# Splitting two late stores into halves in a channel shuffle kernel bound by its DMA engines

## The chip, the cores and the metric

The kernel runs on one core of a Trainium2 chip. The metric is the device time of one execution in microseconds (us), as a median of several runs. A ratio of two kernels is the mean time of one kernel's fast runs over that of the other's of the same rounds, with a 95% interval; it is not quite the ratio of the medians that are quoted. Executions over 1.5% slower than the fastest of the same kernel are left out of the means. A gain or loss counts as such from 2% on. Single times of a trace are given to 0.01 us, some of them cut and not rounded.

## The reference, cut to what matters

```python
batch, h, w, c = 16, 64, 64, 256
groups = 8
x = x.reshape(batch, h, w, groups, c // groups)
x = x.transpose(0, 1, 2, 4, 3)          # (group, channel) -> (channel, group)
return x.reshape(batch, h, w, c)        # float32
```

The input has 67.11 MB and the output as many. Each pixel's 256 channels are permuted; nothing is added or multiplied.

## The kernel before

```python
_SIZES = [4, 8, 16] + [32] * 15 + [4]     # pixels of each of 128 partitions in a tile
_IN_BUFS = 3
_OUT_BUFS = 3
...
    first = 0
    for q in _SIZES:
        in_tile = in_pool.tile([P, biggest * c], F32, name="in_tile")
        nc.sync.dma_start(out=in_tile[:, : q * c], in_=rows(x_flat, first, q))
        out_tile = out_pool.tile([P, biggest * c], F32, name="out_tile")
        nc.vector.tensor_copy(
            out=out_tile[:, : q * c].rearrange("p (i j g) -> p i j g", j=CPG, g=G),
            in_=in_tile[:, : q * c].rearrange("p (i g j) -> p i j g", g=G, j=CPG),
        )
        nc.scalar.dma_start(out=rows(out_flat, first, q), in_=out_tile[:, : q * c])
        first += P * q
```

There are 19 tiles, numbered from 0. SyncE issues a load for each, VectorE copies it with the permutation, and ScalarE issues its store. A partition of a full tile (q = 32) is one row of 32 KB that is contiguous in memory; a tile with q = 4 has rows of 4 KB. Below, L18 and S18 are the load and the store of tile 18.

Of the kernel before, what the change touches and what calls it, by code (L numbers as in the profile page):

```python
# [1 line left out]

# [4 lines left out]


F32 = mybir.dt.float32
P = 128  # L10

_SIZES = [4, 8, 16] + [32] * 15 + [4]
_IN_BUFS = 3
_OUT_BUFS = 3


@with_exitstack
def kernel(  # L18
    ctx: ExitStack,
    tc: tile.TileContext,  # L20
    x: bass.AP,
    groups: bass.AP,
    out: bass.AP,
):
    nc = tc.nc
    b, h, w, c = x.shape
    G = int(groups)
    CPG = c // G
    assert G * CPG == c
    assert sum(_SIZES) * P == b * h * w  # L30
    biggest = max(_SIZES)

    x_flat = x.rearrange("b h w c -> (b h w c)")
    out_flat = out.rearrange("b h w c -> (b h w c)")

    in_pool = ctx.enter_context(tc.tile_pool(name="in_pool", bufs=_IN_BUFS))
    out_pool = ctx.enter_context(tc.tile_pool(name="out_pool", bufs=_OUT_BUFS))

    def rows(flat, first, q):

        return flat[first * c : (first + P * q) * c].rearrange("(p f) -> p f", p=P)

    ctx.enter_context(tc.manual_schedule(engines=None))
    first = 0
    for q in _SIZES:
        in_tile = in_pool.tile([P, biggest * c], F32, name="in_tile")
        nc.sync.dma_start(out=in_tile[:, : q * c], in_=rows(x_flat, first, q))  # L47
        out_tile = out_pool.tile([P, biggest * c], F32, name="out_tile")
        nc.vector.tensor_copy(  # L49
            out=out_tile[:, : q * c].rearrange("p (i j g) -> p i j g", j=CPG, g=G),  # L50
            in_=in_tile[:, : q * c].rearrange("p (i g j) -> p i j g", g=G, j=CPG),
        )
        nc.scalar.dma_start(out=rows(out_flat, first, q), in_=out_tile[:, : q * c])
        first += P * q


# [1 line left out]
_INS = ['x', 'groups']  # L58
_OUTS = [((16, 64, 64, 256), 'float32')]

_NUMBERS = {'groups': 8}


# [26 lines left out]
```

## Time and profile before

| What | Value | Where it is read |
|---|---|---|
| time | 316.96 us (316.69 to 317.02, 3 runs) | runs |
| span of the profiled run | 315.2 us | page, headline |
| two DMA queues | 49.8% + 49.4% of 16 engines | page, DMA queues |
| VectorE | 38% busy | page, busy shares |
| L18, issue to landing | 42.1 us | chain of waits |
| S18, issue to landing | 14.9 us | DMA issues from 299.2 us on |

The page's part on DMA issues gives, for each kind of DMA, the queue, the count, the size and the median time from issue to landing:

```profile
in_tile<-in_x_dram SPq DMA_DIRECT2D x15, 4096.0 KB, 50.5
out_dram<-out_tile ACTq DMA_DIRECT2D x15, 4096.0 KB, 42.4
```

A full tile is 4096 KB and would take 4.19 MB / 432 GB/s = 9.7 us alone. That it takes 42 to 50 us says that several stand in line on each queue.

### The profile page before, as it was taken

The numbers are of one execution on the slowest core, as the hardware profiler recorded it, in microseconds if no ns is written. First come the engines' busy times: TensorE is split into PE (matmuls) and PEld (weight loads), VectorE is DVE, ScalarE is ACT, GpSimd is POOL, SyncE is SP. The second block draws the span as 40 slices with busy tenths as digits, with TensorE's granted clock in tenths as the row PEclk, the third lists the DMA queues.
The fourth block names the chain that finished last, engine by engine and source line by source line (L and its number), as shares of the span: only waits on it lengthen the run. The fifth ranks groups of instructions, "written<-read, shape, count | busy, mean of one in ns | idle before, by whom it ended". The sixth has DMA issues, their size and how long they took to land.

```text
span 315.2 us, 150 instructions
## 1 busy us (share of the span) xinstructions
DVE 119.9 (38%) x19; POOL 0.2 (0%) x4
## 2 busy tenths in 40 slices
DVE  2419270905318062270722608135090440905500
POOL 0000000000000000000000000000000000000000
DMA  8999999999999999999999999999999999999996
GB/s 314 408 422 458 403 449 408 457 408 453 412 453 412 458 412 453 420 445 428 437 428 437 437 428 437 428 437 433 437 433 437 428 441 424 445 420 426 439 441 291
DMA packets 5472, 134.22 MB, mean 426 GB/s; under 512 B 608, under 2 KB 608, under 8 KB 1120
## 3 DMA queue, kind: packets, MB, share of 16 engines
q1 hardware_dynamic: 2736, 67.11, 49.8%
q10 hardware_dynamic: 2736, 67.11, 49.4%
HBM read 67.11 MB, written 67.11 MB: 426 GB/s over the span
## 4 chain that ended last, share of the span: by engine, by line
DMA 40%; another core or an unknown queue 30%; DVE 25%; issue 0%; DVEq 0%; SPq 0%
DMA in_tile<-in_x_dram 40%; DVE out_tile L49 25%; DVEq L49 0%; SPq L47 0%
## 5 line engine op out<-in xcount | busy, mean ns | idle before, releaser
L49 DVE COPY out_tile<-in_tile 128x8192 f32<-128x8192 f32 (+3 forms) x19 | 119.9, 6313 | 179.3 <-DMA in_tile<-in_x_dram 179.3
L71 POOL MEMSET const-uint8-127<- 128x1 uint8 x1 | 0.1, 103 | 0.0
L71 POOL MEMSET const-bfloat16-1.0<- 128x1 bf16 x1 | 0.1, 102 | 0.0
L71 POOL MEMSET const-float32-0.0<- 128x1 f32 x1 | 0.1, 99 | 0.2 <-issue 0.2
L71 POOL MEMSET const-float32-1.0<- 128x1 f32 x1 | 0.1, 99 | 0.0
## 6 DMA issues: line engine op xcount, KB each, us to landing
in_tile<-in_x_dram SPq DMA_DIRECT2D x15, 4096.0 KB, 50.5
out_dram<-out_tile ACTq DMA_DIRECT2D x15, 4096.0 KB, 42.4
in_tile<-in_x_dram SPq DMA_DIRECT2D x1, 2048.0 KB, 11.1
out_dram<-out_tile ACTq DMA_DIRECT2D x1, 2048.0 KB, 30.1
in_tile<-in_x_dram SPq DMA_DIRECT2D x2, 512.0 KB, 22.7
in_tile<-in_x_dram SPq DMA_DIRECT2D x1, 1024.0 KB, 5.5
out_dram<-out_tile ACTq DMA_DIRECT2D x2, 512.0 KB, 14.4
out_dram<-out_tile ACTq DMA_DIRECT2D x1, 1024.0 KB, 22.9
```

The costliest lines, as they stand in the source:

```text
L49: nc.vector.tensor_copy(out=out_tile[:, : q * c].rearrange("p (i j g) -> p i j g", j=CPG, g=G), in_=in_tile[:, : q * c].rearrange("p (i g ...
L71: nc = _bacc.Bacc("TRN2", target_bir_lowering=False, num_devices=1)
```

## The change

Its intent is that the last large stores leave in smaller pieces, so that the small load and store behind them get through earlier.

```diff
+_HALVED = (16, 17)
...
-    for q in _SIZES:
+    for t, q in enumerate(_SIZES):
...
-        nc.scalar.dma_start(out=rows(out_flat, first, q), in_=out_tile[:, : q * c])
+        n = 2 if t in _HALVED else 1
+        for k in range(n):
+            cols = slice(k * q // n * c, (k + 1) * q // n * c)
+            nc.scalar.dma_start(
+                out=rows(out_flat, first, q)[:, cols], in_=out_tile[:, cols]
+            )
```

## The prediction

> **What bounds the kernel now.** I read the page's headline and busy shares first, then the forty slices, the table of DMA queues, the groups by shape, the DMA issues, and at the end the chain of waits.
>
> ```profile
> span 315.2 us, 150 instructions
> DVE 119.9 (38%) x19; POOL 0.2 (0%) x4
> DMA  8999999999999999999999999999999999999996
> q1 hardware_dynamic: 2736, 67.11, 49.8%
> q10 hardware_dynamic: 2736, 67.11, 49.4%
> ```
>
> VectorE, the only engine that computes, is busy for 38% of the span. The DMA engines are at 9 tenths or more in every slice but the first and the last, and the two queues (q1 carries the loads, q10 the stores) together fill 49.8 + 49.4 = 99.2% of sixteen engines' time. So the kernel is bound by its DMA engines: 134.22 MB go through them and nothing else counts unless it leaves them without work.
>
> The stretches at the end, cut at the times that matter below (columns: stretch, its length, busy DVE, busy POOL, clock, DMA share, GB/s), say that this holds until the last two microseconds:
>
> ```profile
> 280.00:287.00 7.00, 0.00 (x0) 0.00 (x0) 1.00 1.00 432
> 287.00:292.40 5.40, 5.17 (x1) 0.00 (x0) 1.00 1.04 445
> 292.40:298.00 5.60, 2.30 (x1) 0.00 (x0) 1.00 0.99 424
> 298.00:303.00 5.00, 1.09 (x1) 0.00 (x0) 1.00 1.00 433
> 303.00:312.40 9.40, 0.00 (x0) 0.00 (x0) 1.00 0.94 407
> 312.40:315.20 2.80, 0.00 (x0) 0.00 (x0) 1.00 0.32 132
> ```
>
> The share stays at 0.94 to 1.04 up to 312.4 us; there is no gap that an earlier store could fill. The last stretch holds the small last store, its landing and the closing barrier.
>
> The chain of waits ends with a piece that looks like a target for this change:
>
> ```profile
> 255.96 42.12 DMA in_tile<-in_x_dram
> 298.08 0.03 issue
> 298.11 0.05 DVEq L49
> 298.15 0.04 issue
> 298.20 1.09 DVE out_tile L49
> ```
>
> The load of the last, small tile (512 KB) is issued at 255.96 and lands only at 298.08. I number tiles from 0, as the code does: tile 18 is this one, tiles 16 and 17 are the ones whose stores are halved, L and S are loads and stores. The landing records of the trace (sixteen semaphore steps for each DMA; I quote the ninth as the middle and the sixteenth as the last) give L17 at 287.15 last, so 10.9 us pass between two landings for 512 KB. The DMA records explain it: one record of a 32 KB row takes 1213 ns on its engine, one of 4 KB 159 ns, and each engine takes one row of the load queue and one of the store queue in turn. L18 has 8 rows of 4 KB on each engine: 8 x (0.159 + 1.213) = 10.98 us. But while it waits its turn the engines move store rows, so this wait costs the bound nothing.
>
> **What the Trainium skill says.** "DMA: Bandwidth & Descriptors", section "Queues, rings and completion order", has each DMA engine go round-robin between the queue rows at the granularity of packets, of several descriptors. The trace agrees on the taking of turns and shows turns of a single row: besides the 10.9 us above, S1 (8 KB rows) and S2 (16 KB rows) landed beside loads of 32 KB rows 14.82 us apart in the middle, and 8 x (0.611 + 1.213) = 14.59. The same page, "Where 436 GB/s comes from", puts the ceiling at 435 GB/s; here a 32 KB row in 1213 ns is 27.0 GB/s for an engine, 432 for sixteen, which is the 432 of the stretch above. Its section "Why small descriptors are slow" tells of a fixed cost for each packet: the trace has medians of 159, 309, 611 and 1213 ns for 4, 8, 16 and 32 KB, so a row cut in two costs 2 x 611 - 1213 = 9 ns more. "Trainium Kernel Development and Optimization", "Key Constraints", says that DMAs from all issuing engines share the same 16 DMA engines; the shares of q1 and q10 add up to 99.2% here, which agrees.
>
> **The change part by part.** Removed: two stores of 4096 KB with rows of 32 KB. Added: four of 2048 KB with rows of 16 KB. No byte, VectorE instruction or load is added.
>
> Part 1, **time on the DMA engines**. On each engine 16 rows of 1213 ns (two stores, 8 rows each) become 32 rows of 611 ns: 16 x 9 = 144 ns more. Two more DMAs mean two more semaphore writes on each engine, 9 ns each by the records: 18 ns. Sum: +0.16 us, all of it on the bound, as the engines have no gap.
>
> Part 2, **the issues**. Two more store issues on ScalarE's queue, each of 338 to 380 ns. S16 is issued at 275.3, and its rows start after S15's middle landing at 292.40; S17 is issued at 294.73, and its rows start after S16's middle landing at 302.76. So the second halves are in the queue some 7 to 16 us before their turn. Cost: 0.
>
> Part 3, **new waits**. The built program uses eight DMA semaphores in turn, and two DMAs more shift those after them. By the order of instructions with their waits, the halves wait for old loads and for S12 and S14, the last of which landed at 279.03: done before the issues that name them. One is real: L18 now also waits for S13, which landed at 259.63, where it was issued at 255.96. It goes out 3.7 us later. Its rows can move only after L17's, whose middle landing is 286.83: 27 us of slack. Cost: 0.
>
> Part 4, **the taking of turns**. This is the visible gain. Up to S15's end at 292.40 L18 makes (292.40 - 286.83) / 1.372 = 4 of its 8 turns against 32 KB rows, as before. The other 4 are now beside 16 KB rows: 4 x (0.159 + 0.611) = 3.08 us in place of 4 x 1.372 = 5.49. L18 should land 2.4 us earlier, near 295.7, VectorE should then copy tile 18 from about 295.8 to 296.9 (it ends tile 17 at 294.7, so it is free), and S18 should be issued at about 296.9 and not at 299.31. But S18 stands behind S17 in the same queue, and S17's rows run until 312.44. What is gained is more waiting in the queue. Gain at the end: 0.
>
> Part 5, **the closing waits**. SyncE waits at the end for the eight semaphores in four pairs. Before, S18's was in the second pair, so two pairs were still to be passed after its landing at 314.21, about 62 ns each by the trace. In the changed program it is in the last pair: -0.12 us.
>
> Sum: +0.16 + 0 + 0 + 0 - 0.12 = +0.04 us. 316.96 + 0.04 = **317.0 us**.
>
> **The rivals.**
> - *The earlier last store shortens the end.* It would be 2.4 us if S18's issue at 299.31 set the end: 314.6 us, 0.8% faster, and still within 2%. For it speaks the chain of waits, which ends at tile 18's copy. Against it speaks that S18's issue takes 14.9 us to land, for 512 KB which need 8 x 0.159 = 1.27 us on an engine, and that the share stays near 1 from 298 to 312.4. I give it 4%.
> - *Shorter rows lose bandwidth.* A row's record is measured at 611 ns only for S2, beside loads. If 16 KB pieces with a pitch of 32 KB wrote 10% slower to HBM, 8.4 MB at 432 GB/s are 19.4 us, so +1.9 us: 318.9 us. For it: the pieces of a half aren't contiguous, as S2's rows are. Against: a row is still 16 KB long, and 8 KB rows reach 309 ns, 98% of the rate of a long row. I give a visible loss 6%.
> - *A new wait starves a queue.* If a half had to wait for a DMA that is late, or ScalarE's queue held only so many DMAs, S17's second half would come late. S17 has rows for 9.7 us, so a delay has to pass several microseconds before an engine idles. If S17's second half waited for S16's end at 303.3 it would still be in time. 2%, and it would make 317 to 319 us.
>
> **Range and chances.** The three runs before lie between 316.69 and 317.02, so their spread is 0.33 us, larger than any term of my sum. The range of eight in ten is that spread on either side of 317.0, a little wider above for the second rival: **316.5 to 317.6 us**. Crossing 2% takes 6.3 us, which neither rival reaches: faster 0.01, within 2% 0.98, slower 0.01.
>
> **What would show the steps right or wrong.** In the changed profile, the number of DMA packets should be 5472 + 16 x 16 + 2 x 16 = 5760, and 16 KB store rows should have a median of 611 ns (part 1). L18 should be issued near 259.7 and land near 295.7; tile 18's copy should start near 295.8 and not 298.20; S18's issue should be near 296.9 and its time to landing should grow from 14.9 to about 17.5 us (parts 3 and 4). The stretches from 280 to 312 us should keep a share near 1. The prediction is wrong if the share sinks there by more than a few hundredths, if the 16 KB store rows take well over 611 ns, or if S17 lands before 312, which would say that the bytes moved faster.

## The result, and the profile after

The changed kernel takes 316.75 us (316.63 to 317.15, 6 runs), the kernel before beside it 316.69 us (316.46 to 317.02, 6 runs). The ratio is 1.0001, with an interval of 0.9988 to 1.0014: the same. All these runs are fast ones.

The page of the changed kernel, headline, busy shares, packets and queues:

```profile
span 314.9 us, 152 instructions
DVE 121.0 (38%) x19; POOL 0.2 (0%) x4
DMA packets 5760, 134.22 MB, mean 426 GB/s; under 512 B 640, under 2 KB 640, under 8 KB 1152
q1 hardware_dynamic: 2736, 67.11, 49.8%
q10 hardware_dynamic: 3024, 67.11, 49.5%
```

The store queue (q10) has 3024 records where it had 2736: 256 for the rows cut in two and 32 for the semaphore writes of two DMAs more. Its share grew from 49.4% to 49.5%. The DMA engines are as full as they were, and the bytes are the same, so the time is the same.

The stretches at the end of the changed kernel, with the columns of the prediction's table:

```profile
280.00:287.00 7.00, 0.00 (x0) 0.00 (x0) 1.00 1.04 448
287.00:292.40 5.40, 3.75 (x1) 0.00 (x0) 1.00 0.92 394
292.40:298.00 5.60, 4.80 (x2) 0.00 (x0) 1.00 0.99 421
298.00:303.00 5.00, 0.00 (x0) 0.00 (x0) 1.00 1.02 436
303.00:312.40 9.40, 0.00 (x0) 0.00 (x0) 1.00 0.99 422
```

The third stretch now holds two VectorE copies (tile 17's end and tile 18's), and the fourth none: tile 18's copy has moved forward. The shares change a little from stretch to stretch, as a long record counts whole in the stretch in which it starts. Over the whole 32.4 us the share is 0.99 in both kernels, and the mean rate is 425 GB/s where it was 426.

The last pieces of the chain of waits after:

```profile
218.78 40.48 DMA out_dram<-out_tile
259.25 0.02 SPq L49
259.27 0.03 issue
259.31 37.18 DMA in_tile<-in_x_dram
296.48 0.03 issue
...
296.60 1.10 DVE out_tile L51
```

Two things are new in it. A store stands ahead of L18, which now goes out at 259.31, when S13 has landed, and not at 255.96. And although L18 goes out 3.4 us later, it lands 1.6 us earlier: at 296.48 and not at 298.08. For what follows, the answer on DMA issues between 296 and 298.2 us shows S18:

```profile
out_dram<-out_tile ACTq DMA_DIRECT2D x1, 512.0 KB, 16.4
```

It was issued at 297.73 where it was 299.31, and it lands at 314.14 where it was 314.21. So 1.58 us of a head start became 1.5 us more in line, 16.4 for 14.9 us, and next to nothing at the end.

### The profile page after: what moved, and what is told of

Its sections match the earlier page's. It is cut to its first block, busy times and chain, and to the rows that moved or that the text cites. A ratio compares the mean times of both kernels' runs of the same rounds, so it can differ in the third digit from the quotient of the medians.

```text
span 314.9 us, 152 instructions
## 1 busy us (share of the span) xinstructions
DVE 121.0 (38%) x19; POOL 0.2 (0%) x4
## 2 busy tenths in 40 slices
DMA packets 5760, 134.22 MB, mean 426 GB/s; under 512 B 640, under 2 KB 640, under 8 KB 1152
## 3 DMA queue, kind: packets, MB, share of 16 engines
q1 hardware_dynamic: 2736, 67.11, 49.8%
q10 hardware_dynamic: 3024, 67.11, 49.5%
## 4 chain that ended last, share of the span: by engine, by line
DMA 51%; another core or an unknown queue 22%; DVE 20%; issue 0%; DVEq 0%; SPq 0%
DMA in_tile<-in_x_dram 38%; DVE out_tile L51 20%; DMA out_dram<-out_tile 13%; DVEq L51 0%; SPq L49 0%
```

## The experiments

The theory: the DMA engines have work from the start to 312 us, so the time is the sum of the rows on an engine, and S18's issue may move freely as long as it is in line before S17 ends. The first rival: an earlier S18 is worth its time, and the shorter rows cost as much, so the two cancel in the changed kernel. The second: short rows, or the waits that come with more DMAs, are expensive, and two tiles of them are too few to see.

Each run is stated beside runs of the kernel before on the same chip, whose medians lie between 316.66 and 316.75 us. All gave the right result.

### late_2 and late_3: S18 goes out later

```diff
+        if t == 18:
+            for _ in range(2):                # late_3: 3
+                nc.vector.tensor_copy(
+                    out=out_tile.rearrange("p (i j g) -> p i j g", j=CPG, g=G),
+                    in_=last.rearrange("p (i g j) -> p i j g", g=G, j=CPG),
+                )
+        last = in_tile
```

> The kernel before, with VectorE copying tile 17 twice more, into the output buffer of tile 18, ahead of tile 18's copy (which then overwrites it; the result stays right). S18's issue moves from 299.3 to about 310.7 us, where S17's rows still run until 312.4. My theory: nothing changes, 0.0 to 0.3 us over the kernel before. Rival (S18's issue sets the end): 11 us slower.

> The same with three added copies: S18's issue at about 318.2 us, after S17's rows have ended at 312.4. Now the DMA engines run dry. My theory: S18 lands about 2.7 us after its issue, near 321 in place of 314.2, so about 6.8 us slower. Rival (S18's issue sets the end everywhere): 19 us slower.

`late_2` took 316.75 us, ratio 0.9999 (0.9984 to 1.0014). `late_3` took 323.64 us, ratio 1.0218 (1.0204 to 1.0232), which is 6.9 us more. The timeline of `late_2` at the end:

```profile
294.58 15.05 DVE L51 COPY out_tile<-in_tile 128x8192 f32<-128x8192 f32 x2
294.74 16.38 ACTq L60 DMA_DIRECT2D out_dram<-out_tile  x2
309.67 1.08 DVE L56 COPY out_tile<-in_tile 128x1024 f32<-128x1024 f32 x1
```

and that of `late_3`:

```profile
294.75 22.32 DVE L51 COPY out_tile<-in_tile 128x8192 f32<-128x8192 f32 x3
294.89 23.69 ACTq L60 DMA_DIRECT2D out_dram<-out_tile  x2
317.11 1.10 DVE L56 COPY out_tile<-in_tile 128x1024 f32<-128x1024 f32 x1
```

In `late_2` tile 18's copy starts 11.5 us later than in the kernel before and S18 goes out at 310.78, yet it lands at 314.26, as before (314.21). In `late_3` it goes out at 318.24, after S17 has landed at 312.80, and lands 2.65 us later at 320.89; the DMA share from 312.40 us to the end of the span is 0.14 there. So S18's issue has over 11 us of slack. This settles the first rival: what the change gains lies inside slack that is free anyway. It also shows that the method sees a late issue when there is one.

### halve_16 and halve_17: one half of the change each

```diff
-_HALVED = (16, 17)
+_HALVED = (16,)      # halve_17: (17,)
```

> Only tile 16's store is halved. My theory: L18 takes its last four turns beside 16 KB rows, so it lands at a middle of about 295.4 us, as in the changed kernel, and S18 goes out at 297 to 298; the time stays at that of the kernel before plus 0.0 to 0.1 us. Rival (an earlier S18 is worth its time and the short rows cost as much): half of the cost is gone and the whole gain is there, so 0.5 to 1.2 us faster.

> Only tile 17's store is halved. My theory: L18 has all its turns beside 32 KB rows, so its middle landing is about 297.8 and S18 goes out near 299.3, as in the kernel before; the time stays within 0.1 us of it. Rival (an earlier S18 is worth its time and the short rows cost as much): half of the cost without the gain, so 0.5 to 1.2 us slower.

`halve_16` took 316.74 us, ratio 1.0 (0.9987 to 1.0013), and `halve_17` 316.80 us, ratio 1.0003 (0.999 to 1.0016). Tile 18's copy in the timeline of `halve_16`:

```profile
295.98 1.09 DVE L51 COPY out_tile<-in_tile 128x1024 f32<-128x1024 f32 x1 [1.10 <-DMA in_tile<-in_x_dram]
```

and in that of `halve_17`:

```profile
298.29 1.09 DVE L51 COPY out_tile<-in_tile 128x1024 f32<-128x1024 f32 x1 [3.51 <-DMA in_tile<-in_x_dram]
```

The whole head start comes from tile 16's halves: L18's middle landing is 295.56 us in `halve_16` and 297.74 in `halve_17`, where the kernel before has 297.75. L18 takes its last turns beside S16's rows, not beside S17's. The times don't differ. `halve_16` leaves no room for the 0.5 us of gain that the rival needs, and `halve_17` hardly any for its 0.5 us of loss.

### rows_16k and rows_4k: what a cut row costs

```diff
+    def pieces(flat, first, q):
+        if q < 32:
+            return rows(flat, first, q)
+        part = flat[first * c : (first + P * q) * c]
+        return part.rearrange("(k p f) -> p k f", k=K, p=P)   # K = 2; rows_4k: K = 8
...
-        nc.scalar.dma_start(out=rows(out_flat, first, q), in_=out_tile[:, : q * c])
+        nc.scalar.dma_start(out=pieces(out_flat, first, q), in_=cut(out_tile, q))
```

The load is cut in the same way, and `cut` gives the tile in K pieces for each partition.

> Loads and stores of all full tiles have rows of 16 KB instead of 32 KB, in one DMA each: 38 DMAs and the waits of the kernel before, so row length alone. The tile takes other rows of the array, loads and stores alike. My theory: 30 x 8 x 9 ns = 2.2 us slower, ratio 1.007. Rival (short rows lose bandwidth, some 10%): 30 us slower.

> The same with rows of 4 KB. My theory, from the 159 ns of a 4 KB row in the kernel before: 8 x 159 - 1213 = 59 ns more for each 32 KB, 30 x 8 x 59 ns = 14.2 us slower, ratio 1.045. If the rows of so short a length wait on one another more than the records of the small tiles showed, it is slower still.

`rows_16k` took 317.77 us, ratio 1.0034 (1.0021 to 1.0046), and `rows_4k` 325.52 us, ratio 1.0276 (1.0262 to 1.029). The first is 1.0 us slower, which is clear of the noise but far under 2%, where I had expected 2.2 us; the second is 8.8 us slower, where I had expected 14.2. The page of `rows_4k`:

```profile
DMA packets 32352, 134.22 MB, mean 414 GB/s; under 512 B 608, under 2 KB 608, under 8 KB 31840
q1 hardware_dynamic: 16176, 67.11, 50.9%
q10 hardware_dynamic: 16176, 67.11, 50.2%
```

The shares add up to 101.1%, so records overlap: a record's length is longer than the step to the next one. I put the records of the kernel before on sixteen engines, each after the one that ends nearest to its start; there a record starts 4 ns before the one ahead of it ends (median). Rows of 32, 16 and 4 KB then step by 1209, 607 and 155 ns, and a cut costs 2 x 607 - 1209 = 5 ns, not 9. The runs agree: 1.04 us for 240 cut rows on an engine is 4.3 ns a cut (the interval allows 2.8 to 6.1), and 8.79 us for 240 x 7 cuts is 5.2 ns. The second rival falls for rows alone. (The short rows of these two runs lie next to each other in memory; halves with gaps between them are those of `halve_16` and `halve_17`.)

### halve_all: every full tile in halves

```diff
-_HALVED = (16, 17)
+_HALVED = tuple(range(3, 18))
```

> All fifteen full tiles leave as two halves. My theory (the DMA engines are full, a cut row costs 9 ns, a DMA more costs one semaphore write of 9 ns on each engine): 15 x 8 x 9 ns = 1.08 us for the rows and 15 x 9 ns = 0.14 us for the semaphore writes, so about 1.2 us over the kernel before, ratio 1.004; 16 KB store rows at a median of 611 ns. Rival (the halves lose bandwidth, and the earlier last store hides it in the changed kernel): the earlier last store could hide at most 2.4 us of loss for two tiles, so up to 1.2 us a tile, 18 us less 2.4 for fifteen: up to 15 us slower. Rival (the added waits are harmless only because they were old): with every tile halved most loads wait for a store, and the loads come late; several us slower, with a DMA share below 0.95 in the middle.

This missed. `halve_all` took 328.85 us (325.35 to 330.44), ratio 1.036 (1.0321 to 1.0398): 12 us more by the medians, ten times what my theory gave. One of its six runs, of 330.44 us, counts as slow, and the ratio is of the other five. The waits of SyncE's queue (line and what was waited for; us in total, times, longest):

```profile
SPq L49 <- DMA out_dram<-out_tile: 261.5, 13, 28.6
```

and the page's DMA issues of `halve_all`:

```profile
out_dram<-out_tile ACTq DMA_DIRECT2D x31, 2048.0 KB, 46.0
in_tile<-in_x_dram SPq DMA_DIRECT2D x15, 4096.0 KB, 20.7
```

Three DMAs a tile turn eight semaphores over so fast that from L7 on each load waits for a store of four tiles earlier; in all 13 loads wait for a store, where the changed kernel has one. A load lands 20.7 us after its issue and not 50.5, so SyncE has little in line. Still, no engine idles in the middle: the sum of busy records is 16 of 16 up to 310 us. Two other things grew. One is **slow rows**: the time by which records exceed the typical one of their size is 1.3 us for an engine in the kernel before, nearly all in the first 50 us, and 5.2 us here, 3.9 of them after the first 50 us, with single load rows up to 2484 ns where 1213 is typical. The other is **engines drifting apart**: the last store's sixteen landings go from 315.21 to 324.57, a spread of 9.4 us where the kernel before has 0.8, and the last engine sets the end. The ninth of these landings is at 318.02 us, where it was 313.67: of the 10.4 us by which the last one comes later, 4.4 thus fall on the middle engine too, and the rest is drift. One suspected cause was the waits; another was that load rows of 32 KB in turn with store rows of 16 KB give the loads two thirds of an engine's time. The next two runs have one each.

### one_dma_16k and extra_dma: the short rows alone, the waits alone

```diff
-        out_tile = out_pool.tile([P, biggest * c], F32, name="out_tile")
+        gap = 16
+        out_tile = out_pool.tile([P, 2 * (16 * c + gap)], F32, name="out_tile")
...
+            halves = out_tile.rearrange("p (k f) -> p k f", k=2)[:, :, : 16 * c]
...
+            nc.scalar.dma_start(
+                out=rows(out_flat, first, q).rearrange("p (k f) -> p k f", k=2),
+                in_=halves,
+            )
```

> The short store rows of halve_all without its added DMAs: each full tile leaves in one DMA, but the output tile has a gap of 64 bytes in its middle, so its rows are 16 KB (VectorE copies it in two parts). DMAs and semaphore waits are those of the kernel before. Theory W (halve_all's 12 us come from the load issues that wait for a store's semaphore): about 15 x 8 x 5 ns = 0.6 us slower, at most 1.5, and loads land about 50 us after their issue. Theory T (they come from the taking of turns: against 16 KB rows the loads get two thirds, run ahead, and the load queue runs dry): 8 to 14 us slower, with slow load rows and a growing spread of a store's sixteen landings, as in halve_all.

```diff
         nc.scalar.dma_start(out=rows(out_flat, first, q), in_=out_tile[:, : q * c])
+        if q == 32:
+            spare = spare_pool.tile([16, 128], F32, name="spare")
+            nc.scalar.dma_start(out=spare, in_=rows(x_flat, 0, 32)[:16, :128])
```

> The waits of halve_all without its short rows: stores are whole, with 32 KB rows, and after each full tile's store ScalarE issues one load of 8 KB into spare buffers, so there are 3 DMAs a tile as in halve_all and the load of a tile waits for a store of four tiles earlier. Theory W: 6 to 14 us slower, loads landing some 20 us after their issue. Theory T: 0.1 to 0.5 us slower.

`one_dma_16k` took 317.60 us, ratio 1.0028 (1.0016 to 1.0041), 0.9 us more. `extra_dma` took 318.05 us, ratio 1.0044 (1.003 to 1.0058), 1.4 us more. Neither theory stands as the one cause. The DMA issues of `one_dma_16k`:

```profile
in_tile<-in_x_dram SPq DMA_DIRECT2D x15, 4096.0 KB, 22.6
out_dram<-out_tile ACTq DMA_DIRECT2D x15, 4096.0 KB, 46.6
```

and those of `extra_dma`:

```profile
in_tile<-in_x_dram SPq DMA_DIRECT2D x15, 4096.0 KB, 27.6
out_dram<-out_tile ACTq DMA_DIRECT2D x15, 4096.0 KB, 49.2
```

What SyncE's queue waited for most, in `one_dma_16k`:

```profile
SPq L47 <- DVE out_tile L59: 219.6, 13, 27.6
```

and in `extra_dma`:

```profile
SPq L49 <- DMA spare<-in_x_dram: 205.1, 10, 22.4
```

So `extra_dma` has such waits as `halve_all`, but not the same ones: ten loads waited for a spare load, which stands in line behind a store, and only one for a store itself. In `one_dma_16k` VectorE copies each full tile in two parts, and the loads waited for it.

In both the loads run ahead and few stand in line, nearly as in `halve_all`, and yet slow rows cost only 1.4 and 2.1 us on an engine (0.7 us of the latter in one spell near 131 us) and the last store's landings spread by 0.6 and 0.7 us. So a thin load queue costs little by itself. `halve_all`, which has both, is 12 us slower where the parts sum to 2.3. It differs from both in one thing more, which no run has alone for all tiles: the two halves of a row leave in different DMAs. What makes the rows slow and the engines drift is left open.

### full_16, start_28 and start_16: other sizes of tile

```diff
-_SIZES = [4, 8, 16] + [32] * 15 + [4]
+_SIZES = [32] * 16                     # full_16
+_SIZES = [28] + [32] * 15 + [4]        # start_28
+_SIZES = [16] + [32] * 15 + [16]       # start_16
```

> Sixteen full tiles and no small ones, 32 DMAs. My theory: the time on each DMA engine is the sum of its rows, 256 x 1213 ns + 32 x 9 ns = 310.8 us where the kernel before has 311.3, and no engine starves since the loads have three buffers ahead at the start and a whole store in the queue at the end. So 0.4 to 0.6 us faster, ratio 0.9985. Rival (the small tiles at the ends shorten the start and the tail): without the small first tiles the first store starts some 13 us later, without the small last one the last store starts 7.5 us after the last load; up to several us slower.

> The first three tiles (4, 8, 16) of the kernel before made one of 28; the sixteen other tiles have the rows and addresses that they had. It asks why full_16 was 7.4 us slower. If the large first tile is the cause (all engines start their first stores together and beside loads of equal rows): 5 to 8 us slower, with slow load rows through the whole run, as in full_16. If the addresses of full_16's tiles (whole multiples of 4 MB) or its large last tile are the cause: within 1 us of the kernel before.

> Tiles of 16, fifteen times 32, and 16: one first tile as in start_28, but smaller. In full_16 and start_28 the slow rows go with a fixed step between the two streams: a load's first landing comes some 17 us after a store's, or 2.4 us before the next one's, so both queues begin their tiles together; in the kernel before it comes 9 us after, half a tile. Theory P (this step matters): worked through with the rows' times, the step here is about 6 us, so no slow rows after the start, and 0.0 to 0.5 us faster than the kernel before by the rows' sum. Theory F (a run without the small first tiles is slow, whatever the step): 3 to 15 us slower, with slow load rows through the whole run.

`full_16` was to be the version that beats both, since it has the fewest rows, and it missed: 324.15 us, ratio 1.0235 (1.0221 to 1.0248). Its slow rows cost 6.5 us on an engine (1.5 of them in the first 50 us, where the kernel before has 1.3), in groups at every new tile through the run. Besides, its engines stand idle for 1.4 us on average from 306.4 to 309.6 us: its last store goes out only at 308.68 us, when the first engines have run out of rows. That is a part of the expected rival, that the small last tile shortens the tail.

`start_28` took 323.19 to 336.11 us; with this spread three of its four runs count as slow ones, and no ratio is given. Its fastest run, a single one, is 6.5 us over the kernel before, which is in the 5 to 8 us expected of a large first tile, and not within the 1 us expected if the addresses or the large last tile of `full_16` were the cause.

`start_16` took 316.90 us, ratio 1.0006 (0.9993 to 1.002): the same, with no slow rows after the first 30 us, though it lacks the small first tiles as well. So theory F of that run falls. Theory P is not proved either: the step between a store's first landing and a load's next one is 3.5 us in `start_16`, not the 6 that I had worked out, 9 us in the kernel before, and 17 us in `full_16` and `start_28`. Slow rows after the start went with the 17 us in two kernels and were absent at 3.5 and 9; four kernels that agree with a guess are a correlation, and of one of them, `start_28`, the trace is of a slow run (331.13 us). No version tried beats the kernel before.

## Why the prediction was right or wrong

It was right in the time, 317.0 us against 316.75. The difference that it forecast, +0.04 us, and the measured one of the medians, +0.06 us, are both too small for the runs to tell from zero; that they agree is luck as far as the single terms go, and those have to be checked in the traces.

- **What bounds the kernel** holds: `late_2` moves an issue by 11 us without effect, and `late_3` shows the effect once the engines run dry.
- **Part 1, rows.** The mechanism was right and the size was off: I took records of 9 ns more for steps of 9 ns more. The runs with cut rows give 4.3 to 5.2 ns a cut, so 16 cuts cost about 0.08 us and not 0.14. In the traces S18's middle landing moved from 313.66 to 313.77, which is 0.11 us with everything in it. The number of records, 5760, is the one foretold, and 16 KB store rows have the median of 611 ns.
- **Part 2, issues.** The second halves were in line long before their turn: that of S16 for 20.7 us and that of S17 for 11.1, counted from the issue to the middle landing of the first half. The prediction's 7 to 16 us were counted to the turn of the first halves. This cost nothing, as said.
- **Part 3, new waits.** L18 went out at 259.3 us and not at 259.7, released by S13 as foretold, at no cost. For two tiles the step is right. As a rule for more tiles it would have failed: in `halve_all` such waits and short rows together cost 12 us.
- **Part 4, turns.** L18's middle landing moved from 297.75 to 295.41 us, 2.34 us earlier where I had 2.4. The last of its sixteen landings, the one that the prediction put near 295.7, is 296.48, as some engines were behind in that run: L17's landings spread over 2.8 us there and 1.2 us before. `halve_16` is without this, and L18's last landing is 295.86 in it. S18's issue thus came at 297.73 and not at 296.9, and its wait in line is 16.4 us and not 17.5.
- **Part 5, closing waits.** From S18's last landing to the end of SyncE's waits it is 0.08 us, before it was 0.21: 0.13 us less, where I had 0.12.
- **A sign of being wrong that came up.** The share from 287.00 to 292.40 us is 0.92 and was 1.04, which is more than the few hundredths that the prediction allowed. The stretch before it rose from 1.00 to 1.04 and that from 303.00 to 312.40 us from 0.94 to 0.99, and over all of them it is 0.99 in both kernels. So the engines did not run dry; stretches of 5 us were too short for this sign. The others did not come up: S17 landed at 312.91 us, and the 16 KB store rows took 611 ns.

The sum, +0.08 for rows, about 0.01 for two semaphore writes (an estimate: two records of 9 ns, each less the 4 ns by which records overlap) and -0.13 for the closing waits, is nothing that the runs could tell from zero. The rival of an earlier last store is refuted by `late_2`; that of slow short rows by the changed kernel's own trace, in which the 512 half rows took 611 ns in the median and 629 at most, and by `rows_16k` and `one_dma_16k`. That of a starved queue did not occur with two tiles: the engines had work throughout.

## What to carry to other kernels

Where, as here, the DMA engines are full and a queue always has a store in line, moving an issue forward only lengthens its stay in line. Ask first how far the issue can be delayed without effect: as long as a later issue costs nothing, an earlier one can't gain anything. Compare the time from issue to landing with the time that the bytes need: 14.9 us for 1.27 us of rows says that the issue isn't the limit. And a split that is free for two tiles need not be free for all: here more DMAs brought waits on reused semaphores, and `halve_all` cost more than the sum of the parts that were tried.

## What the Trainium skill lacked or had wrong

- "DMA: Bandwidth & Descriptors", section "Queues, rings and completion order": it has an engine drain a packet of several descriptors before it turns to the other queue. Here each turn is one row, of 4 KB as of 32 KB: eight turns of L18 beside a store's 32 KB rows took 10.9 us, and 8 x (0.159 + 1.213) is 10.98. Of how many descriptors such a row is made isn't shown.
- The same page, "Why small descriptors are slow": it has a fixed overhead of about 3 cycles for each packet, in an example of 256 bytes, and no time for long rows. The runs give 4.3 ns for each cut from 32 to 16 KB rows and 5.2 ns for each from 32 to 4 KB, and show that a record's length overstates the step to the next by about 4 ns.
- The same page, "Where 436 GB/s comes from": its note says that for transfers between HBM and SBUF the HBM side, about 358 GB/s, binds, as half of what two cores share, and does not say there that a core alone gets more, as the skill has it elsewhere. On this single core loads and stores together reached 426 GB/s over the span and 432 in stretches, with records of 27 GB/s on each engine, both directions taken together; this is near the page's 435. No run here has two cores at work.
- No page has it for rows that lie next to each other: rows that take up to twice their usual time, 2484 ns and not 1213, while all sixteen engines are busy. They cost 5.2 us on an engine in `halve_all` and 6.5 us in `full_16`, of which 1.2 and 1.5 fall in the first 50 us, where the kernel before has 1.3 as well; what sets them off is open.
- No page has it: that DMAs which reuse eight semaphores in turn make a load's issue wait for an older store. It was one load of 19 with two stores split, and 13 with fifteen.
